# Routing of two token tiles: residual stream and statistics per half, and a gate ahead of the second half of the first tile's routing

## The chip, the cores and the metric

One core of one Trainium2 chip runs the kernel. The metric is device time in microseconds of one execution, median of three runs. Instructions of one engine run in the order in which the program lists them; the engines (TensorE = PE, VectorE = DVE, ScalarE = ACT, GpSimd = POOL, SyncE = SP, which issues the weight loads) wait for one another by semaphores.

## The reference, cut to what matters

256 tokens pass two hybrid layers and then a block with a state-space branch, a pooling branch, and a mixture of experts. The change lies between the block's output projection and its experts:

```python
xl = post_norm(xl, mod_l[2] * out_l, ln1_g, ln1_b)      # layer_norm(ALPHA * x + gate * out)
hl = modulate(xl, mod_l[3], mod_l[4]).reshape(b * l, d)
lg = hf @ w_rg + b_rg                                   # 4 group logits
grp = argmax(lg)
le = (hf @ w_re[grp]) + b_re[grp]                       # 8 expert logits of that group
top_v, top_i = top_k(le, 2)                             # two experts per token
```

Each token then goes through its two experts out of 32 (1024 to 512 to 1024), and the weighted sum is added to the stream.

## The kernel before, in words

The tokens lie in two tiles of 128 partitions, t = 0 and t = 1, and every product of 1024 output columns is cut in two halves of 512, n = 0 and n = 1.

**Output projection (in `mix`, "wout").** Four accumulators `po[t][n]` take the four PSUM buffers of pool `pa`. After the first half of the reduction is done for all four, the rest comes tile by tile: t = 0 with n = 0 and n = 1, then t = 1 with n = 0 and n = 1. Each of the four is 4 calls of `mm3`, and one `mm3` is 3 matmuls of 512 columns.

**Routing (`pre`, one task per tile).** Its steps, with the lines that the trace shows:

1. Stream and statistics: per half a product with the gate row (L1881), the sum into the stream (L1882) and `bn_stats` (L1884; L1838 for the second half), then `bn_aggr` and two small operations on DVE (L1839 to L1843) and two on POOL (L1844, L1847), which give 1/sigma and -mean/sigma.
2. Eight transposes of the stream on PE (L337) into two buffers of PSUM pool `pt` (which has two), four copies to SBUF on ACT (L1892), and a small product on DVE (L1895).
3. The logits: 8 float32 matmuls (the trace shows 16 passes, `pb_wout` for t = 0, `pb_pre` for t = 1); then the normalised stream (L1903 on DVE for t = 0, L1901 on ACT for t = 1), its rounded copy (L1904, ACT) and, for t = 0, the remainder (L1937, DVE).
4. `route`: the first maximum and the group (L1954 to L1972), then the second maximum (L1963 again, to L1976). L1975 writes the assignment `Asg`.
5. Slots and gather: `Asg` matmuls for the positions (`pt_pre`, `pb_pre`), then L1920 and L2029 on DVE make the selection matrix, and 16 matmuls of 256 columns (`pa_pre`) gather the tile's tokens into four accumulators that reuse the buffers of `po`. After those of t = 1 the result is copied out (L2094, L2096), and the experts begin (`pb_moe`, L2124).

**What sets the order.** The instructions are listed by a small planner at build time. A task is a Python generator; `self.clk` counts planned PE time; `yield c` makes the task due `c` units later, and `poll`, at the end of every `mm3`, lets each due task list its next step. `join` goes on with the task that is due first until the named one is done. `YPRE = (2.0, 1.3, 0.6, 0.2)` are the delays behind the steps 1, 2 and 3 and in the middle of `route` (the last two for t = 0 alone). In these units an `mm3` counts 0.64, a transpose 0.21, and a logits matmul 0.107. The dictionary `self.sc` gets a tile's statistics at the end of step 3, and task 0 stands before its step 5 until tile 1's are there (`while 1 not in self.sc: yield 0.5`). A buffer goes to a new tile once the last use of the old one, as listed, is over.

**Behind it.** `pre_end` computes the weights of the experts. Then 16 pairs of experts follow, each with 12 weight blocks of 1 MB that SP streams through a ring of buffers; a load is listed when the matmuls that free its buffer are. SP's queue is in order too.

Of the kernel before, what the change touches and what calls it, by code (L numbers as in the profile page):

```python
# [13 lines left out]
OP = mybir.AluOpType  # L14
# [13 lines left out]
ALPHA = 2.0 ** 0.25  # L28
# [26 lines left out]
YPRE = (2.0, 1.3, 0.6, 0.2)  # L55
# [179 lines left out]
class Emit:  # L235
# [214 lines left out]
    def m(self, n=512, dt=F32):  # L450

        self.n += 1
        return self.mp.tile([P, 512], dt, tag="m", name=f"m_{self.n}")[:, :n]
# [1122 lines left out]
    def mix(self):  # L1576
        nc, A, m = self.nc, self.A, self.m
# [149 lines left out]
        for k, u in MIX_ORDER:  # L1727
# [19 lines left out]
            if u < 8 and u % 2:  # L1747
                g = u // 2
# [8 lines left out]
        po = [[self.pA() for _ in range(2)] for _ in range(2)]  # L1757
        for j in range(8):
# [6 lines left out]
            for i in range(2):  # L1765
                hi, lo = self.half(("vba", j), i)
                for k in range(8):
                    kk = 8 * i + k
                    c = slice(k * P, (k + 1) * P)
# [14 lines left out]
        tp = []  # L1784
        for t in range(2):
            sl = slice(t * P, (t + 1) * P)
            for n in range(2):
                for k in range(4):
                    hi, lo = w[2 * n + k // 2]
                    c = slice((k % 2) * 512, (k % 2 + 1) * 512)  # L1790
                    self.mm3(po[t][n], mx.h(4 + k)[:, sl], mx.l(4 + k)[:, sl], hi[:, c], lo[:, c], False, k == 3)
            tp.append(self.spawn(self.pre(po, t)))
        self.done(4)
        self.prefetch(RING_C + NSPL)
        self.ph = "pre"
# [54 lines left out]
    def pre_start(self):  # L1850

        m, small = self.m, self.small
        self.yT = [m().rearrange("p (k s) -> p k s", k=2) for _ in range(4)]
        self.nh, self.nl = ([self.a4(n, F32R) for _ in range(2)] for n in ("yh", "yl"))
        self.G, self.posm = (self.mw.tile([P, 2, 32], F32, name=n) for n in ("G", "posm"))
        self.asg = self.mw.tile([P, 2, 32], F32R, name="Asg")
        self.mxc = self.mw.tile([P, 1], I32, name="mxc")

        r = self.rt = m(512)

        nc, self.rows = self.nc, r[:, 384:512]
        nc.gpsimd.memset(self.rows, 0.0)
        nc.gpsimd.dma_start(self.rows[0:16], self.A["rows"][4:6, :].rearrange("a (k p) -> (a k) p", p=P))
        nc.gpsimd.dma_start(self.rows[16:24], self.md_dram[1])
        self.gl, self.el, self.v0, self.v1, self.gmx, self.og = (
            r[:, a:b].rearrange("p (t e) -> p t e", t=2) for a, b in ((0, 8), (8, 72), (72, 80), (80, 88), (88, 90), (90, 98)))
        self.o = [r[:, a:a + 64].rearrange("p (t e) -> p t e", t=2) for a in (98, 162)]
        self.rc, self.rb, self.rg = (r[:, a:b].rearrange("p (t e) -> p t e", t=2) for a, b in ((226, 290), (290, 362), (362, 380)))  # L1870
        self.Q0 = m(dt=F32R).rearrange("p (t s) -> p t s", t=2)
        self.sc = {}

    def pre(self, po, t):

        nc, x = self.nc, self.x[t]
        st = self.small(2, 6)
        for n in range(2):
            c = slice(n * 512, (n + 1) * 512)
            g = self.m()  # L1880
            nc.vector.tensor_tensor(g, po[t][n], self.gate_row[:, c], op=OP.mult)  # L1881
            nc.vector.scalar_tensor_tensor(x[:, c], x[:, c], ALPHA, g, op0=OP.mult, op1=OP.add)  # L1882
            if n == 0:
                nc.vector.bn_stats(st[:, 0, :], x[:, c])  # L1884
        nm, r = sc = self.stats_end(st, x[:, 512:])
        yield YPRE[0]
        for q in range(2):
            ps = self.pT()
            for k in range(4):
                self.tr(ps[:, k * P:(k + 1) * P], x[:, (4 * q + k) * P:(4 * q + k + 1) * P])  # L1890
            for k in range(2):
                nc.scalar.activation(self.yT[2 * q + k][:, :, t * P:(t + 1) * P],  # L1892
                                     ps[:, 2 * k * P:2 * (k + 1) * P].rearrange("p (k s) -> p k s", k=2), AF.Copy)

        nc.vector.scalar_tensor_tensor(self.rb[:, t], self.wsum, nm, self.rsm[:, R_BR:R_BR + 36], op0=OP.mult, op1=OP.add)  # L1895
        yield YPRE[1]
        pl = self.pB()
        for k in range(8):
            self.mm(pl[:, :36], self.yT[k // 2][:, k % 2, t * P:(t + 1) * P], self.vr[:, k * 36:(k + 1) * 36], k == 0, k == 7)
        if t:  # L1900
            nc.scalar.activation(x, x, AF.Identity, scale=r, bias=nm)  # L1901
        else:
            nc.vector.tensor_scalar(x, x, r, nm, op0=OP.mult, op1=OP.add)  # L1903
        nc.scalar.activation(self.nh[t], x, AF.Copy)  # L1904
        if t == 0:
            self.low_part(t)
        self.sc[t] = sc
        yield YPRE[2] if t == 0 else 0.0
        yield from self.route(t, pl, r)
        if t == 0:  # L1910
            while 1 not in self.sc:
                yield 0.5
            self.pn, self.pp = self.pB(), self.pT()
            self.mm(self.pp[:, 0:32], self.sbr, self.asg[:, 0])
            self.mm(self.pp[:, 32:64], self.onr, self.asg[:, 0], True, False)
            self.mm(self.pn[:, 0:32], self.onr, self.asg[:, 0], True, False)
        else:
            self.mm(self.pp[:, 32:64], self.sbr, self.asg[:, 1], False, True)
            self.mm(self.pn[:, 0:32], self.onr, self.asg[:, 1], False, True)
        nc.vector.tensor_tensor(self.posm[:, t], self.posm[:, t], self.pp[:, 32 * t:32 * t + 32], op=OP.add)  # L1920
        self.slots(0, (t,), self.Q0)
        if t:
            self.low_part(t)
        if t == 0:
            self.xg0 = self.slots_input()
            self.pg = [self.pA() for _ in range(4)]
        for y in (self.nh, self.nl):
            for k in range(8):
                kb = slice(k * P, (k + 1) * P)
                o = self.pg[k // 2][:, k % 2 * S:(k % 2 + 1) * S]  # L1930
                self.mm(o, y[t][:, kb], self.Q0[:, t], t == 0 and y is self.nh and k % 2 == 0, t == 1 and y is self.nl and k % 2 == 1)
                if t and y is self.nl and k % 2:
                    for i in (k - 1, k):
                        self.channels(self.xg0(i), self.pg[k // 2][:, i % 2 * S:(i % 2 + 1) * S], i)
# [4 lines left out]
    def route(self, t, ps, r):  # L1939

        nc = self.nc
        tt, stt, red = nc.vector.tensor_tensor, nc.vector.scalar_tensor_tensor, nc.vector.tensor_reduce

        def g4(v):
            return v.rearrange("p (g e) -> p g e", e=8)

        def b8(v):
            return v[:, :, None].to_broadcast([P, 4, 8])

        rb, gl, el = self.rb[:, t], self.gl[:, t], g4(self.el[:, t])  # L1950
        c, b, cg, bg = g4(self.rc[:, t]), self.rg[:, t, 0:4], self.rg[:, t, 4:8], self.rg[:, t, 8:9]
        gmx, og = self.gmx[:, t], self.og[:, t]
        o = [g4(x[:, t]) for x in self.o]
        stt(self.el[:, t], ps[:, 4:36], r, rb[:, 4:36], op0=OP.mult, op1=OP.add)  # L1954
        stt(gl, ps[:, 0:4], r, rb[:, 0:4], op0=OP.mult, op1=OP.add)

        group = [lambda: red(gmx, gl, axis=AX.X, op=OP.max),
                 lambda: tt(cg, gl, gmx.to_broadcast([P, 4]), op=OP.is_equal),
                 lambda: stt(cg, cg, -64.0, self.io8[:, 0:4], op0=OP.mult, op1=OP.add),
                 lambda: red(bg, cg, axis=AX.X, op=OP.min),  # L1960
                 lambda: tt(og, cg, bg.to_broadcast([P, 4]), op=OP.is_equal)]
        for i, v in enumerate((self.v0[:, t], self.v1[:, t])):
            for f in (lambda: red(v, el, axis=AX.X, op=OP.max),  # L1963
                      lambda: tt(c, el, b8(v), op=OP.is_equal),
                      lambda: stt(c, c, -64.0, self.io8[:, None, :].to_broadcast([P, 4, 8]), op0=OP.mult, op1=OP.add),
                      lambda: red(b, c, axis=AX.X, op=OP.min),
                      lambda: tt(o[i], c, b8(b), op=OP.is_equal)):
                f()
                if group:
                    group.pop(0)()  # L1970
            if i == 0:
                stt(el, o[0], -3e38, el, op0=OP.mult, op1=OP.add)  # L1972
                yield YPRE[3] if t == 0 else 0.0
        tt(c, o[0], o[1], op=OP.add)
        tt(g4(self.asg[:, t]), c, b8(og), op=OP.mult)  # L1975
        nc.vector.tensor_scalar(self.posm[:, t], self.asg[:, t].bitcast(F32), -1e6, 1e6, op0=OP.mult, op1=OP.add)  # L1976
# [425 lines left out]
```

## Time and profile before

| what | value |
|---|---|
| runs | 1620.33 us median of 3 (1618.15 to 1621.02) |
| profiled execution | 1620.23 us, span 1618.5 us |
| PE busy | 1534.4 us, 95% of the span |
| DVE busy | 938.1 us, 58% |
| ACT busy | 641.3 us, 40% |
| moved from HBM | 406.15 MB, 253 GB/s over the span |
| stretch of the change | from about 1107 to 1135 us of the span |

The span is the part of the execution in which instructions ran; 1.73 us of the profiled execution lie outside it. A row of the timeline gives start, time from the first start to the last end of the merged instructions, engine, line, operation, output and inputs, count, and in brackets the idle time of the engine before it with what ended that. A line such as L330 or L337 is that of a helper; the name of the output tells what it was called for.

### The profile page before, as it was taken

The page shows a single profiled execution, that of the slowest core. Times are in us where ns is not written, and L with a number is a line of the kernel's source. Part 1 is how long each engine was busy: PE and PEld are TensorE (multiplying, and loading weights), DVE is VectorE, ACT ScalarE, POOL GpSimd, SP SyncE. Part 2 cuts the span into 40 slices and gives each one's busy share as a digit, 9 for nine tenths or more (in the row PEclk, how much of TensorE's full clock was granted, in tenths as well). Part 3 has the DMA queues.
Part 4 walks back from the last instruction along what each step waited for, and adds up shares of the span by engine and source line. Part 5 has one row for each costly group of instructions (what it writes and reads, how often), then busy time and mean ns, then how long its engine had stood idle before and what let it go on. Part 6 is the DMA issues. An engine that isn't in the chain of part 4 may idle for free.

```text
span 1618.5 us, 23434 instructions
## 1 busy us (share of the span) xinstructions
PE 1534.4 (95%) x9319; PEld 1172.6 (72%) x9319; DVE 938.1 (58%) x1670; ACT 641.3 (40%) x1103; POOL 37.8 (2%) x55
## 2 busy tenths in 40 slices
PE   7999999999999999998899999998999999989886
PEld 6888999999889999998777779997544444434332
DVE  6768787658777777579899875466321112111103
ACT  5646544446556444456545545442211111111100
POOL 1000000000000000000000000000000000000000
PEclk9999999999999999999999999998999999999998
DMA  8655666644455666644433235588699999999996
GB/s 331 225 197 220 221 231 248 242 172 156 138 176 181 228 227 254 224 150 160 167 124 114 98 117 183 192 315 325 236 365 410 411 410 411 412 412 410 411 412 245
DMA packets 90251, 411.16 MB, mean 254 GB/s; under 512 B 10520, under 2 KB 15568, under 8 KB 62216
## 3 DMA queue, kind: packets, MB, share of 16 engines
q1 hardware_dynamic: 83032, 401.12, 65.6%
q0 software_dynamic: 2464, 6.37, 1.2%
q10 hardware_dynamic: 4640, 2.12, 0.4%
q8 instruction: 75, 1.23, 0.3%
q14 instruction: 40, 0.33, 0.1%
HBM read 406.15 MB, written 3.94 MB: 253 GB/s over the span
## 4 chain that ended last, share of the span: by engine, by line
PE 70%; DVE 13%; DMA 12%; ACT 2%; issue 2%; POOL 1%; SPq 0%; DVEq 0%; ACTq 0%; POOLq 0%
PE pb_ff L330 16%; PE pb_moe L2124 10%; PE pa_ff L330 8%; PE pa_z L330 7%; PE pb_gate L330 4%; DMA w<-in_weu_dram 4%; DMA w<-in_wed_dram 4%; PE pb_moe L2174 3%; DVE lo L376 3%; PE pb_br L330 3%; DMA w<-in_weg_dram 2%; DVE m L1267 2%; PE pa_zz L330 2%; PE pa_uu L330 2%; PE pa_wo L330 2%
## 5 line engine op out<-in xcount | busy, mean ns | idle before, releaser
L376 DVE TENSOR_TENSOR lo<-raw,hi 128x1024 fp32r<-128x1024 f32 (+2 forms) x334 | 383.6, 1165 | 31.3 <-ACT hi L389 31.2
L389 ACT ACTIVATE hi<-raw 128x1024 fp32r<-128x1024 f32 (+2 forms) x334 | 335.4, 1008 | 143.7 <-PE pa_z L330 46.1
L2124 PE MATMUL pb_moe<-w,xg 128*64 128x512 f32 x960 | 240.1, 596 | 10.5 <-DMA w<-in_weg_dram 10.3
L330 PE MATMUL pb_ff<-hh,hi 128*128 128x256 f32 x704 | 200.6, 285 | 0.0
L330 PE MATMUL pb_ff<-hl,hi 128*128 128x256 f32 x704 | 199.1, 283 | 0.0
L330 PE MATMUL pb_ff<-hh,lo 128*128 128x256 f32 x704 | 199.1, 283 | 0.0
L2124 PEld LDWEIGHTS pb_moe<-w,xg 128*64 128x64 f32 x960 | 74.3, 137 | 140.3 <-issue 108.9
L470 ACT ACTIVATE m<-m 128x256 fp32r<-128x256 f32 (+1 forms) x76 | 38.3, 504 | 282.9 <-DVE m L2180 184.7
L330 PEld LDWEIGHTS pb_ff<-hh,hi 128*128 128x128 f32 x704 | 134.7, 191 | 1.1
L330 PEld LDWEIGHTS pb_ff<-hl,hi 128*128 128x128 f32 x704 | 134.7, 191 | 1.0
L330 PEld LDWEIGHTS pb_ff<-hh,lo 128*128 128x128 f32 x704 | 134.7, 191 | 0.0
L2174 PE MATMUL pb_moe<-w,m 128*64 128x512 f32 x472 | 120.8, 596 | 12.4 <-DMA w<-in_wed_dram 12.3
L2094 DVE TENSOR_SCALAR xg<-pt_moe,rsm 128x256 f32<-128x256 f32 x28 | 13.9, 540 | 182.1 <-PE pt_moe L2159 182.1
L330 PE MATMUL pa_ff<-hi,m 128*128 128x512 f32 x352 | 116.0, 397 | 0.0
L2174 PEld LDWEIGHTS pb_moe<-w,m 128*64 128x64 f32 x472 | 38.6, 137 | 83.2 <-issue 54.8
L330 PE MATMUL pa_z<-hi,hh 128*128 128x384 f32 (+1 forms) x256 | 94.5, 369 | 0.2 <-ACT hi L389 0.2
L330 PE MATMUL pa_z<-lo,hh 128*128 128x384 f32 (+1 forms) x256 | 88.9, 347 | 0.3 <-DVE lo L376 0.3
L1267 DVE SCALAR_TENSOR_TENSOR m<-m,fx 128x254 f32<-128x254 f32 (+1 forms) x176 | 85.0, 483 | 7.0 <-ACT m L1255 2.1
L330 PE MATMUL pa_z<-hi,hl 128*128 128x384 f32 (+1 forms) x256 | 88.6, 346 | 0.0
L330 PEld LDWEIGHTS pa_ff<-hi,m 128*128 128x128 f32 x352 | 66.2, 188 | 15.1
L330 PE MATMUL pa_ff<-lo,m 128*128 128x512 f32 x176 | 70.0, 397 | 0.0
L2180 DVE TENSOR_TENSOR m<-pb_moe,gm 128x512 f32<-128x512 f32 x31 | 21.4, 692 | 81.9 <-PE pb_moe L2174 78.8
(539 smaller groups left out, 3001.0 us busy)
## 6 DMA issues: line engine op xcount, KB each, us to landing
raw<-in_wgu_dram SPq DMA_DIRECT2D x44, 1024.0 KB, 5.3
w<-in_wed_dram SPq DMA_DIRECT2D x84, 512.0 KB, 10.2
w<-in_weu_dram SPq DMA_DIRECT2D x82, 512.0 KB, 9.0
w<-in_weg_dram SPq DMA_DIRECT2D x78, 512.0 KB, 10.2
raw<-in_vx_dram SPq DMA_DIRECT2D x22, 1024.0 KB, 5.0
raw<-in_wdn_dram SPq DMA_DIRECT2D x22, 1024.0 KB, 4.9
raw<-in_wza_dram SPq DMA_DIRECT2D x27, 768.0 KB, 4.6
w<-in_weg_dram SPq DMA_DIRECT2D x20, 1024.0 KB, 13.8
```

Source lines behind the costliest of these rows:

```text
L330: self.nc.tensor.matmul(out, l, r, start=start, stop=stop)
L376: self.nc.vector.tensor_tensor(lo, src, hi.bitcast(F32), op=OP.subtract)
L389: self.nc.scalar.activation(hi, s, AF.Copy)
L470: self.nc.scalar.activation(hi, src, AF.Copy)
L1267: nc.vector.scalar_tensor_tensor(acc[:, o0:o1], u[:, o0 + d:o1 + d], w, acc[:, o0:o1], op0=OP.mult, op1=OP.add)
L2094: self.nc.vector.tensor_scalar(dst, src, g, b, op0=OP.mult, op1=OP.add)
L2124: self.nc.tensor.matmul(ps[64 * i:64 * i + 64, :], xg(kk)[:, o + 64 * i:o + 64 * i + 64], w[i][k], start=kk == 0, stop=kk == 7)
L2174: self.nc.tensor.matmul(pd[64 * i:64 * i + 64, :], fT[:, k * P + 64 * i:k * P + 64 * i + 64], w[i][k], start=k == 0, stop=k == 3)
L2180: self.nc.vector.tensor_tensor(yg, pd, self.gm[:, n * 512:(n + 1) * 512], op=OP.mult)
```

## The change

The stream and statistics of step 1 become a function `pre_half`, which is listed behind the matmuls of each half instead of once behind both. The second maximum of tile 0 is listed only when `self.sc` has an entry of tile 1, and that entry is now written when tile 1's statistics are listed (end of step 1), no longer at the end of step 3. The test before step 5 of tile 0 is unchanged in its text.

```diff
                     self.mm3(po[t][n], mx.h(4 + k)[:, sl], mx.l(4 + k)[:, sl], hi[:, c], lo[:, c], False, k == 3)
-            tp.append(self.spawn(self.pre(po, t)))
+                self.pre_half(po, t, n)
+            tp.append(self.spawn(self.pre(t)))
...
+    def pre_half(self, po, t, n):
+        nc, c = self.nc, slice(n * 512, (n + 1) * 512)
+        g, xv = self.m(), self.x[t][:, c]
+        nc.vector.tensor_tensor(g, po[t][n], self.gate_row[:, c], op=OP.mult)
+        nc.vector.scalar_tensor_tensor(xv, xv, ALPHA, g, op0=OP.mult, op1=OP.add)
+        if n == 0:
+            self.st[t] = self.stats_begin(xv)
+
+    def pre(self, t):
         nc, x = self.nc, self.x[t]
-        st = self.small(2, 6)
-        for n in range(2):
-            c = slice(n * 512, (n + 1) * 512)
-            g = self.m()
-            nc.vector.tensor_tensor(g, po[t][n], self.gate_row[:, c], op=OP.mult)
-            nc.vector.scalar_tensor_tensor(x[:, c], x[:, c], ALPHA, g, op0=OP.mult, op1=OP.add)
-            if n == 0:
-                nc.vector.bn_stats(st[:, 0, :], x[:, c])
-        nm, r = sc = self.stats_end(st, x[:, 512:])
+        nm, r = self.sc[t] = self.stats_end(self.st[t], x[:, 512:])
         yield YPRE[0]
...
         if t == 0:
             self.low_part(t)
-        self.sc[t] = sc
         yield YPRE[2] if t == 0 else 0.0
         yield from self.route(t, pl, r)
...
             if i == 0:
                 stt(el, o[0], -3e38, el, op0=OP.mult, op1=OP.add)
-                yield YPRE[3] if t == 0 else 0.0
+                while t == 0 and 1 not in self.sc:
+                    yield 0.2
```

## Rows read from the trace of the kernel before

**Rows 1.** The page's part on the chain that ended last, by engine.
```profile
PE 70%; DVE 13%; DMA 12%; ACT 2%; issue 2%; POOL 1%; SPq 0%; DVEq 0%; ACTq 0%; POOLq 0%
```

**Rows 2.** Stretches of 10 us: busy time by engine, then clock, DMA share, GB/s.
```profile
1130.00:1140.00 10.00, 9.26 (x57) 6.30 (x58) 7.75 (x31) 3.07 (x8) 0.00 (x0) 0.94 0.26 77
...
1150.00:1160.00 10.00, 8.53 (x61) 5.96 (x61) 5.33 (x8) 1.19 (x2) 0.00 (x0) 1.00 0.11 41
...
1180.00:1190.00 10.00, 10.00 (x48) 3.31 (x46) 2.67 (x4) 0.63 (x1) 0.00 (x0) 1.00 0.83 247
...
1370.00:1380.00 10.00, 7.42 (x35) 2.29 (x33) 2.77 (x4) 1.26 (x2) 0.00 (x0) 1.00 1.03 402
```

**Rows 3.** Waits of SP's queue, 1080 to 1618 us: total, times, longest.
```profile
SPq L2081 <- PE pb_moe L2124: 29.6, 21, 10.3
```

**Rows 4.** The chain of waits in order of time: start, length, what.
```profile
1115.73 1.72 PE pb_wout L330 x16
...
1123.68 3.26 PE pb_pre L330 x16
...
1128.08 3.55 PE pa_pre L330 x16
...
1132.49 2.25 PE pa_pre L330 x16
1134.74 3.61 PE pb_moe L2124 x16
```

**Rows 5.** Timeline of DVE, 1107 to 1131 us.
```profile
1107.38 0.69 DVE L1881 TENSOR_TENSOR m<-pa_br,gm 128x512 f32<-128x512 f32 x1 [0.40 <-PE pa_br L330]
...
1113.82 0.81 DVE L1903 TENSOR_SCALAR x<-x,sm,sm 128x1024 f32<-128x1024 f32 x1
1115.75 1.23 DVE L1937 TENSOR_TENSOR yl<-x,yh 128x1024 fp32r<-128x1024 f32 x1 [1.13 <-ACT yh L1904]
1117.47 0.25 DVE L1954 SCALAR_TENSOR_TENSOR m<-pb_wout,sm,m 128x32 f32<-128x32 f32 x1 [0.50 <-PE pb_wout L330]
...
1118.99 0.68 DVE L1881 TENSOR_TENSOR m<-pa_br,gm 128x512 f32<-128x512 f32 x1
...
1121.05 0.67 DVE L1881 TENSOR_TENSOR m<-pa_br,gm 128x512 f32<-128x512 f32 x1
...
1123.58 0.18 DVE L1963 TENSOR_REDUCE m<-m 128x4 f32<-128x32 f32 x1
...
1124.93 0.19 DVE L1975 TENSOR_TENSOR Asg<-m 128x32 fp32r<-128x32 f32 x1
...
1127.38 0.19 DVE L1920 TENSOR_TENSOR posm<-posm,pt_pre 128x32 f32<-128x32 f32 x1 [1.88 <-PE pt_pre L330]
...
1127.94 0.25 DVE L1954 SCALAR_TENSOR_TENSOR m<-pb_pre,sm,m 128x32 f32<-128x32 f32 x1
...
1130.92 0.19 DVE L1975 TENSOR_TENSOR Asg<-m 128x32 fp32r<-128x32 f32 x1
```

**Rows 6.** Timeline of PE, 1112 to 1127 us.
```profile
1112.63 1.04 PE L337 MATMUL pt_wout<-cp,x 128*128 128x128 f32 x8
...
1120.55 0.71 PE L337 MATMUL pt_pre<-cp,x 128*128 128x128 f32 x4 [2.34 <-DVE x L1882]
1122.59 1.09 PE L337 MATMUL pt_pre<-cp,x 128*128 128x128 f32 x4 [1.34 <-DVE x L1882]
...
1126.75 0.59 PE L330 MATMUL pt_pre<-Asg,m 128*128 128x32 f32 x2
```

**Rows 7.** Timeline of ACT: the copies behind the first four transposes of tile 1.
```profile
1121.29 0.66 ACT L1892 ACTIVATE m<-pt_pre 128x256 f32<-128x256 f32 x2 [5.57 <-PE pt_pre L337]
```

**Rows 8.** Stretches of 2 us, the columns of rows 2 (clock third from the end).
```profile
1120.00:1122.00 2.00, 0.71 (x4) 0.42 (x4) 1.93 (x4) 0.66 (x2) 0.00 (x0) 0.74 1.02 418
...
1126.00:1128.00 2.00, 1.55 (x8) 1.44 (x7) 0.59 (x3) 0.87 (x1) 0.00 (x0) 0.50 1.03 412
...
1130.00:1132.00 2.00, 1.75 (x11) 1.65 (x10) 1.41 (x8) 0.00 (x0) 0.00 (x0) 0.70 0.00 0
```

More of the change, by code (lines that the diff above doesn't have):

```diff
@@ L1871, in pre_start @@
         self.Q0 = m(dt=F32R).rearrange("p (t s) -> p t s", t=2)
-        self.sc = {}
-    def pre(self, po, t):
-        nc, x = self.nc, self.x[t]
-        st = self.small(2, 6)
-        for n in range(2):
-            c = slice(n * 512, (n + 1) * 512)
-            g = self.m()
-            nc.vector.tensor_tensor(g, po[t][n], self.gate_row[:, c], op=OP.mult)
-            nc.vector.scalar_tensor_tensor(x[:, c], x[:, c], ALPHA, g, op0=OP.mult, op1=OP.add)
-            if n == 0:
-                nc.vector.bn_stats(st[:, 0, :], x[:, c])
-        nm, r = sc = self.stats_end(st, x[:, 512:])
+        self.sc, self.st = {}, {}
+    def pre_half(self, po, t, n):
[6 more added lines that the diff above has]
+    def pre(self, t):
+        nc, x = self.nc, self.x[t]
+        nm, r = self.sc[t] = self.stats_end(self.st[t], x[:, 512:])
         yield YPRE[0]
```

## The prediction, made before the changed kernel was built or timed

> **What bounds the kernel now.** I read the page first. The chain that ended last runs through PE for 70%, DVE 13%, DMA 12% [rows 1], so a stage counts only where it holds PE up or the weight loads. Then the stretches of 10 us [rows 2]: from 1130 to 1140 the loads move 77 GB/s and from 1150 to 1160 only 41, although 32 experts are still to be fetched, and 247 between 1180 and 1190; by 1370 they run at 402 GB/s, 1.03 of the engines' time, while PE falls to 7.42 of 10 us. So the last part is bound by the loads, but the loads themselves stand still when the experts begin. Why, SP's waits tell [rows 3]: 29.6 us in 21 waits for expert matmuls (L2124), up to 10.3 at once. All buffers are full, and none comes free before the experts' matmuls run. The chain by time gives that start: behind the gather of tile 1 (1132.49, 2.25 us) the experts begin at 1134.74 [rows 4]. Whatever moves 1134.74 moves every later release of a buffer, hence the end, one for one.
>
> The stretch before it is a chain over PE, DVE and ACT. PE waits 2.34 us and 1.34 us for tile 1's stream halves (L1882) [rows 6], does its transposes and its logits, and gathers tile 0 (1128.08, 3.55 us [rows 4]) while DVE routes tile 1: L1954 at 1127.94, `Asg` at 1130.92 + 0.19 = 1131.11 [rows 5]. That gather costs nothing before: it lies beside the route.
>
> **Part 1: tile 0's halves listed earlier.** Nothing. L1881 of tile 0 already starts at 1107.38 on the signal of PE alone [rows 5]; no other work of DVE was listed between the two places.
>
> **Part 2: tile 1's first half listed earlier.** Planned time puts it behind tile 0's transposes, before tile 0's normalised stream. Its three DVE operations take 1121.05 - 1118.99 = 2.06 us [rows 5]. Its matmuls are over when PE begins tile 0's transposes at 1112.63 [rows 6], so DVE runs them at 1113.82, where L1903 stood. L1903, and through ACT's rounded copy L1937, go from 1115.75 to 1117.81; with 1.23 us of L1937, tile 0's route (L1954) starts at 1119.0, not 1117.47: 1.5 later. From there the first half of the route takes 1118.99 - 1117.47 = 1.52, so tile 1's second half starts at 1120.5 and takes 1123.58 - 1121.05 = 2.53 with its statistics; tile 0's second maximum starts at 1123.05 instead of 1123.58, and its `Asg` (1124.93 + 0.19 before) is ready at 1124.6 [rows 5]. By itself a gain of 0.5 us, since the DVE work is the same and only a wait of DVE's (0.50 in the row at 1117.47, and part of that at 1115.75) is used.
>
> **Part 3: the gate.** Before, the test reads: go on when tile 1's logits have been listed. Step through it after the change. Tile 0's route is listed at the last `mm3` and yields, as `self.sc` has no entry 1. Then tile 1's second half and statistics are listed, and the entry is written there. The joins begin with task 0: due 0.2 after, against 2.0 for task 1. It lists its second maximum, as before. But the next test, before step 5, now passes too: the entry is there. So the `Asg` matmuls, L1920, L2029 and all 16 gather matmuls of tile 0 are listed *before* tile 1's transposes and logits. No DMA is moved past anything. On PE tile 1's eight transposes stand behind matmuls that wait for `Asg` of tile 0, and DVE's route of tile 1 waits for PE. In times:
>
> - `Asg` at 1124.6. The `Asg` matmuls start at 1126.75 and L1920 at 1127.38 in the rows, 0.63 [rows 6, 5]; so L1920 at 1125.25. From L1920 to the gather 1128.08 - 1127.38 = 0.70: gather at 1125.95, 3.55 long at the low clock: PE free at 1129.5. Until then PE has been idle since 1120.55 - 2.34 = 1118.2, over 6 us.
> - Tile 1's transposes. The position buffer `pp` now holds one of the two `pt` buffers until tile 1's slots, so the second four wait for ACT's copies of the first four. Low clock: 0.71 + 0.66 [rows 6, 7] and, as an estimate from the gaps 1120.55 + 0.71 to 1121.29, 0.1 of signals, then 1.09: 1132.05. High clock: 1.04 for eight [rows 6], so 0.52 + 0.76 + 0.52: 1131.3.
> - Logits: 3.26 low, 1.72 high [rows 4]: 1135.3 or 1133.0. PE does this while nothing else is left to do on DVE.
> - Route of tile 1: 1131.11 - 1127.94 = 3.17 to `Asg` [rows 5], 0.63 to L1920, 0.70 to the gather: 4.5 us with PE idle. Gather at 1139.8 or 1137.5.
> - Gather of tile 1: 3.55 low, 2.25 high [rows 4]. Experts at 1143.4 or 1139.75, against 1134.74: +8.7 or +5.0.
>
> The unknown is the clock. [...] Transposes and logits, though PE was busy with them, did not bring it back; it came back 3.1 us into the gather. If the new gather of tile 0 does so too, at 1129.05, the transposes and logits are high, but PE then stands idle from 1133.0 on for 4.5 us; before, 2.8 us after PE fell idle it was low. So the last gather is low: 5.0 + 1.3 = +6.3. If the 3.5 us of gather are not enough, it is +8.7. As a further bound, the experts' first matmuls may start low: before, the low level lasted 8.6 us from the work at 1122.59; less the gather's 3.55, 5 us at half rate cost 2.5: +11.2. The lower bound is +5.0, all high. I take +7.5, the middle of 6.3 and 8.7, the two that the rows of this same stretch support.
>
> [...]
>
> **Sum.** 1620.23 (profiled execution: 1618.5 of span and 1.73 around it) + 7.5 = 1627.7. It lies 0.1 us under the runs' median of 1620.33, which changes nothing. Behind 1134.74 the order of the experts and their loads is the same, and the loads' standstill grows by the same 7.5 us.
>
> **Rivals.**
>
> *The order stays* (the change does only what its words say: tile 0's gather is still listed behind tile 1's logits). For it: the test's text is unchanged, and a gather ahead of the transposes is not named. Against it: the entry in `self.sc` is written before both tests. Then tile 1's first transposes run at 1118.2 instead of 1120.55, the second ones start when the second L1882 ends, 0.55 earlier than 1122.59 because L1881 moves from 1121.05 to 1120.5, and the logits, `Asg` and gathers follow: -0.6; if the earlier transposes also kept the clock high, 1.5 on the logits (3.26 against 1.72) and 1.3 on the gather, of which the route of tile 1 hides the latter: -2.1. 1619.6, down to 1618.1. This is the case on the other side: no loss, decided by whether the second test passes. The same would come if PE took ready matmuls past waiting ones: the transposes would slip ahead whatever the list says. [...]
>
> *The loads absorb the delay.* For it: from 1370 the loads run without a pause and PE waits for them [rows 2]. If they had something to fetch while PE is late, the end would not move: 1620.3. Against it: 77 and 41 GB/s at 1130 to 1160, and SP waiting for expert matmuls [rows 2, 3]; they have no free buffer. To absorb half, 3.7 us: 1624.
>
> *The clock decides otherwise.* All high 1625.2, low far into the experts 1631.4: my own range.
>
> **How the numbers follow.** Forecast with its clock bounds 0.88, order stays 0.08, loads absorb 0.04. The likeliest is 1627.7, its range 1624.5 to 1630.5: it leaves out the far end of the clock and the two rivals with no loss, together under 0.2. A difference below 0.2%, 3.2 us, cannot be told from none here. Slower by more: 0.88 and half of the absorbed case, less a little for a forecast at its very lowest, 0.88. Within: 0.09. Faster by more: 0.03, if the order stays and the clock gives back more than I count.
>
> **What would show it.** Right: on PE the first `pa_pre` matmuls stand before `pt_pre` transposes of tile 1; PE idle some 6 us behind `pa_br`, and again about 4 us before the second `pa_pre`; L1954 of tile 1 between 1133 and 1135.5; the experts begin at 1139.8 to 1143.4; the loads idle that much longer, and the later stages are shifted alike. Part 2 is right if L1954 of tile 0 stands near 1119.0 and `Asg` of tile 0 near 1124.6. Wrong: transposes of tile 1 at 1118; experts at 1134; or a late start with the end unmoved.

## The result and the profile after

The changed kernel takes 1628.77 us (median of 7 runs, 1626.03 to 1631.52) against 1620.33 for the kernel before (7 runs): the ratio is 1.0052, interval 1.0039 to 1.0066, some 8.4 us slower. The forecast was 1627.7, slower, with a chance of 0.88. The profiled execution took 1631.4 us with a span of 1629.6; it is one of the longest of the seven.

The chain of waits of the changed kernel, in order of time (start, length, what):

```profile
1125.85 3.75 PE pa_pre L330 x16
1129.60 0.87 PE pt_pre L337 x4
1130.49 0.67 ACT m L1894 x2
1131.21 1.12 PE pt_pre L337 x4
1132.32 3.27 PE pb_pre L330 x16
...
1140.07 3.75 PE pa_pre L330 x16
1143.82 4.42 PE pb_moe L2126 x16
```

Tile 0's gather now stands ahead of tile 1's transposes and logits, each on the path by itself; in [rows 4] the logits came first and the gather lay beside DVE's route. The experts begin at 1143.82 instead of 1134.74. PE and DVE by the timeline of the changed kernel:

```profile
1112.40 1.04 PE L337 MATMUL pt_wout<-cp,x 128*128 128x128 f32 x8
...
1124.45 0.58 PE L330 MATMUL pt_pre<-Asg,m 128*128 128x32 f32 x2 [6.46 <-DVE Asg L1977]
...
1131.21 1.12 PE L337 MATMUL pt_pre<-cp,x 128*128 128x128 f32 x4 [0.75 <-ACT m L1894]
...
1138.85 0.39 PE L330 MATMUL pt_pre<-Asg,m 128*128 128x32 f32 x1 [3.27 <-DVE Asg L1977]
```

```profile
1113.60 0.68 DVE L1879 TENSOR_TENSOR m<-pa_br,gm 128x512 f32<-128x512 f32 x1
...
1118.72 0.24 DVE L1955 SCALAR_TENSOR_TENSOR m<-pb_wout,sm,m 128x32 f32<-128x32 f32 x1
...
1124.11 0.19 DVE L1977 TENSOR_TENSOR Asg<-m 128x32 fp32r<-128x32 f32 x1
...
1135.62 0.25 DVE L1955 SCALAR_TENSOR_TENSOR m<-pb_pre,sm,m 128x32 f32<-128x32 f32 x1 [9.75 <-PE pb_pre L330]
```

The waits have changed sides. PE is idle 6.46 us for tile 0's assignment and 3.27 us for tile 1's; DVE is idle 9.75 us for tile 1's logits, where in [rows 5] its longest wait was 1.88 us and tile 1's L1954 came close behind tile 0's L1920. The first four transposes of tile 1 were ready in those 6.46 us: in e1 below they run at 1117.30. PE did not take them past the matmuls that waited, so the prediction's aside that it might is out. Now the stretches, of 2 us and of 10 us (columns of rows 2, clock third from the end):

```profile
1120.00:1122.00 2.00, 0.00 (x0) 0.00 (x0) 1.93 (x6) 0.00 (x0) 0.00 (x0) 0.90 1.03 416
...
1130.00:1132.00 2.00, 1.25 (x7) 0.85 (x6) 0.00 (x0) 0.66 (x2) 0.00 (x0) 0.50 0.00 0
...
1144.00:1146.00 2.00, 2.00 (x8) 0.50 (x8) 1.70 (x10) 0.93 (x4) 0.00 (x0) 0.63 0.04 8
```

```profile
1130.00:1140.00 10.00, 5.45 (x25) 4.80 (x23) 3.80 (x24) 3.50 (x6) 0.00 (x0) 0.50 0.00 0
1140.00:1150.00 10.00, 9.93 (x46) 6.28 (x48) 5.91 (x23) 3.27 (x9) 0.00 (x0) 0.73 0.28 80
...
1160.00:1170.00 10.00, 8.53 (x59) 5.84 (x60) 5.33 (x8) 1.20 (x2) 0.00 (x0) 1.00 0.11 34
```

The granted clock is 0.50 from about 1121.6 (0.90 in the first row) to 1145.5 (0.63 in the third). The loads do nothing at all from 1130 to 1140 (0 GB/s), and the pattern of [rows 2], 77, then 41 GB/s at 1150, stands ten later: 80, then 34 at 1160.

### The profile page after: what moved, and what is told of

Its sections match the earlier page's. It is cut to its first block, busy times and chain, and to the rows that moved or that the text cites. A ratio compares the mean times of both kernels' runs of the same rounds, so it can differ in the third digit from the quotient of the medians.

```text
span 1629.6 us, 23435 instructions
## 1 busy us (share of the span) xinstructions
PE 1539.0 (94%) x9319; PEld 1176.5 (72%) x9319; DVE 937.7 (58%) x1670; ACT 641.6 (39%) x1103; POOL 38.0 (2%) x55
## 4 chain that ended last, share of the span: by engine, by line
PE 64%; DMA 19%; DVE 13%; ACT 2%; issue 1%; POOL 0%; SPq 0%; DVEq 0%; ACTq 0%; POOLq 0%
PE pb_ff L330 16%; DMA w<-in_weu_dram 8%; PE pa_z L330 8%; PE pa_ff L330 7%; PE pb_moe L2126 6%; DMA w<-in_wed_dram 6%; PE pb_gate L330 4%; DMA w<-in_weg_dram 4%; PE pb_br L330 3%; DVE lo L376 3%; DVE m L1267 2%; PE pa_wo L330 2%; PE pa_zz L330 2%; PE pa_uu L330 2%; PE pb_xs L330 1%
```

## The experiments

Each was timed beside the kernel before, the first four on one chip, the last two on another. The stage is measured within each profile, from the first transposes of tile 0 to the experts' piece of the chain, since the stages ahead of it differ by a microsecond or two between executions.

| kernel | ratio to before | interval | stage, us |
|---|---|---|---|
| before | | | 1134.74 - 1112.63 = 22.1 |
| changed | 1.0052 | 1.0039 to 1.0066 | 1143.82 - 1112.40 = 31.4 |
| e1, test put back | 0.9997 | 0.9989 to 1.0006 | 1133.66 - 1111.88 = 21.8 |
| e2, gate alone | 1.0059 | 1.0044 to 1.0073 | 1141.80 - 1112.10 = 29.7 |
| e3, changed, PE filled | 1.0026 | 1.0017 to 1.0035 | 1139.77 - 1114.24 = 25.5 |
| e4, e1 with 11 matmuls | 1.0003 | 0.9994 to 1.0011 | 1133.74 - 1111.98 = 21.8 |
| e5, e1 with 20 matmuls | 0.9982 | 0.9973 to 0.9991 | 1132.12 - 1112.52 = 19.6 |
| e6, before, 40 matmuls ahead of the experts | 1.0065 | 1.0049 to 1.0081 | 1145.03 - 1113.66 = 31.4 |

**e1: the halves as changed, the second test as before** (`lgt` is a new set, empty at first).

```diff
+        self.lgt.add(t)                     # behind the logits of tile t, where sc was written before
         yield YPRE[2] if t == 0 else 0.0
...
-            while 1 not in self.sc:
+            while 1 not in self.lgt:
                 yield 0.5
             self.pn, self.pp = self.pB(), self.pT()
```

Expected:

> The halves listed early as in the change, but tile 0's gather waits again until tile 1's logits are listed. Theory (the order of the gather on PE is the whole loss): experts start near 1134.0 us of the span, 0.7 before the kernel before, time 1619.6 us, ratio to before 0.9996, not to be told from before. Rival (delaying tile 0's normalised stream and route by 1.2 to 1.5 us is what costs): the time stays above before by that 1.5 us or more, up to the changed kernel's 1628.8.

Measured 1619.65 us, ratio 0.9997: the whole loss is gone. PE of e1:

```profile
1111.88 1.04 PE L337 MATMUL pt_wout<-cp,x 128*128 128x128 f32 x8
...
1117.30 0.60 PE L337 MATMUL pt_pre<-cp,x 128*128 128x128 f32 x4
1121.27 1.09 PE L337 MATMUL pt_pre<-cp,x 128*128 128x128 f32 x4 [3.37 <-DVE x L1880]
1122.15 3.47 PE L330 MATMUL pb_pre<-vr,m 128*128 128x36 f32 x16
...
1126.75 2.07 PE L330 MATMUL pa_pre<-m,yh 128*128 128x256 f32 x8 [0.53 <-DVE m L2032]
```

Transposes, logits, gather, as in [rows 6, 4]. The rival, that tile 0's later normalised stream costs, falls: the displaced operations are here and cost nothing that the time shows. What the early halves gain, 0.3 us in the stage, is below what the time can show.

**e2: the kernel before with the entry written early, nothing else.**

```diff
-        nm, r = sc = self.stats_end(st, x[:, 512:])
+        nm, r = self.sc[t] = self.stats_end(st, x[:, 512:])
...
-        self.sc[t] = sc
```

Expected:

> The kernel before with one thing changed: the statistics entry is written when tile 1's statistics are listed, so tile 0's gather is listed ahead of tile 1's transposes; the halves stay where they were. Theory: nearly the whole loss, and 0.5 more since tile 0's assignment comes 0.5 later: experts near 1144.3, time 1629.3 us, ratio 1.0055. Rival (the moved halves cost): about 1620.3, ratio 1.000.

Measured 1629.07 us, ratio 1.0059: this line is enough for the loss. The profiled execution of e2 is one of the faster ones (span 1625.3); its experts begin at 1141.80, not at the 1144.3 expected. Its chain, and one stretch with the clock, show why:

```profile
1126.15 3.75 PE pa_pre L330 x16
...
1132.16 1.72 PE pb_pre L330 x16
...
1138.37 3.43 PE pa_pre L330 x16
1141.80 3.58 PE pb_moe L2123 x16
```

```profile
1131.00:1132.00 1.00, 0.50 (x4) 0.50 (x5) 0.00 (x0) 0.45 (x2) 0.00 (x0) 0.98 0.00 0
```

The order is that of the changed kernel, but here the clock came back at about 1131.0 (0.98 in the row), in time for the logits (1.72, not 3.27), and was low again in tile 1's gather (3.43). So e2's profile met the 6.3 us case of the forecast and the changed kernel's profile the 8.7 one. That the spread between their runs comes from this is likely, but each has one profile only.

**e3: the changed kernel with PE kept at work.**

```diff
+    def pe_fill(self, n):
+        d = self.pT()
+        for _ in range(n):
+            self.nc.tensor.matmul(d, self.idr, self.nh[0][:, :512], start=True, stop=True)
...
         nm, r = self.sc[t] = self.stats_end(self.st[t], x[:, 512:])
+        if t:
+            self.pe_fill(24)
...                                          # behind the logits
+            self.pe_fill(12)
```

Expected:

> The changed kernel with 24 matmuls of 512 columns put on PE behind the last output projection, and 12 behind tile 1's logits; nobody reads them. [...] Theory with a clock share: logits 3.27 to 1.72, the two gathers 3.75 to 2.25 each, transposes about 0.7 less, experts' first matmuls 0.9 less: 5.5 to 6 less, experts near 1138.5, time 1623 us, ratio 1.0017; what is left of the loss, about 3 to 5 us, is the order alone. Rival (the order alone is the loss and the clock has no share): 1628.8, ratio 1.005.

Measured 1623.65 us, ratio 1.0026, where 1.0017 was expected. The granted clock was 1.00 throughout, and the chain has these lengths:

```profile
1118.00:1128.00 10.00, 8.50 (x45) 6.87 (x45) 7.64 (x32) 1.06 (x1) 0.75 (x2) 1.00 0.99 390
1128.00:1138.00 10.00, 8.14 (x56) 6.95 (x55) 4.37 (x24) 3.50 (x6) 0.00 (x0) 1.00 0.30 120
```

```profile
1127.40 2.17 PE pa_pre L330 x16
1129.58 0.45 PE pt_pre L337 x4
1130.05 0.67 ACT m L1896 x2
1130.76 0.66 PE pt_pre L337 x4
1131.42 1.72 PE pb_pre L330 x16
...
1137.51 2.26 PE pa_pre L330 x16
1139.77 3.60 PE pb_moe L2135 x16
```

The added matmuls do no useful work, yet they give back 0.0026 of the 0.0052: at the high clock the changed kernel is 4.2 us behind the kernel before (2.8 to 5.7). That is not yet the price of the order, since the kernel before pays for the low clock too. The like-for-like pair is e3 and e5 below, both at a granted clock of 1.00 throughout: 1.0026 against 0.9982, some 7 us (5 to 9 by their intervals), and 25.5 against 19.6 us in the stage. Without added matmuls the pair is the changed kernel and e1, both with a stretch at 0.50: 1.0052 against 0.9997, some 9 us (6 to 11), and 31.4 against 21.8 in the stage. So most of the loss is the order by itself; the clock adds 3.7 us by the stages of these profiles and about 2 by the times, which is within their noise.

**e4: e1 with 11 such matmuls between the two fours of tile 1's transposes.**

```diff
         for q in range(2):
+            if t and q:
+                self.pe_fill(11)
             ps = self.pT()
```

Expected (the first kernel is e1, and the theory takes the granted clock to stay at 1.00 with these matmuls):

> [...] Theory: logits 1.72 instead of 3.26 and gather of tile 0 2.25 instead of 3.55, after which DVE sets the pace: experts near 1132.4, 2.3 before the kernel before, time 1618 us, ratio 0.9986. Rival (DVE alone sets the chain here, the clock changes nothing): as the first kernel, 1619.6.

Measured 1620.04 us, ratio 1.0003: a miss. The clock of e4 by stretches, its logits, and the chain:

```profile
1118.00:1122.00 4.00, 3.21 (x18) 2.39 (x17) 3.90 (x18) 0.66 (x2) 0.00 (x0) 1.00 1.03 420
1122.00:1124.00 2.00, 1.69 (x16) 1.59 (x16) 1.73 (x11) 1.35 (x3) 0.75 (x2) 0.93 1.03 416
1124.00:1128.00 4.00, 3.45 (x15) 3.36 (x16) 3.38 (x23) 1.61 (x2) 0.00 (x0) 0.50 1.03 410
```

```profile
1121.82 1.87 PE L330 MATMUL pb_pre<-vr,m 128*128 128x36 f32 x16
```

```profile
1125.34 3.78 PE pa_pre L330 x16
...
1129.98 3.75 PE pa_pre L330 x16
1133.74 3.71 PE pb_moe L2135 x16
```

The logits ran at a granted clock of 1.00 (1.87 us in this view, 3.47 in e1), but it fell to 0.50 at about 1123.7 (0.93 in the second row), behind them, and both gathers ran low: what the logits gained the second gather lost (3.75 against 2.26 in e1). The low stretch was moved, not removed, so this run did not yet tell my theory from the rival.

**e5: 14 matmuls there, 2 behind tile 1's logits, 2 ahead of each gather** (the edit of e4 with 14, and two more lines `pe_fill(2)`, one of which serves both gathers).

Expected:

> As the kernel with the gather back behind the logits and 11 idle matmuls, with 14 of them there, 2 more behind tile 1's logits, and 2 ahead of each gather. In the run with 11 the clock fell to half at 1123.9, behind the logits, and both gathers ran at 3.75 us. Theory (the clock was still the pace there): if it now stays up, the gathers take 2.25, DVE's route of tile 1 sets the pace, and the experts begin 1.8 us earlier than in that run: ratio 0.9988, 1617.7 us. If logits lower the clock whatever stands around them, it falls again and nothing is gained: ratio 1.000. Rival (PE's order and clock have nothing left to give here): no gain although the clock stays up.

Measured 1617.44 us, ratio 0.9982, interval 0.9973 to 0.9991: faster than both kernels. The clock of e5 and the end of its chain:

```profile
1118.00:1128.00 10.00, 9.66 (x62) 7.87 (x60) 9.28 (x48) 3.62 (x6) 0.75 (x2) 1.00 1.02 414
1128.00:1138.00 10.00, 9.09 (x52) 5.33 (x54) 7.38 (x30) 3.59 (x11) 0.00 (x0) 1.00 0.45 141
```

```profile
1128.51 0.20 DVE Asg L1988
1128.71 0.04 issue
1128.76 0.30 PE pt_pre L330
...
1129.87 2.25 PE pa_pre L330 x16
1132.12 3.61 PE pb_moe L2137 x16
```

At a granted clock of 1.00 throughout, tile 1's assignment sets the pace (DVE), and the stage takes 19.6 us, 2.2 less than e1's. So the low clock was what held e1, by some 2.4 us of its time (0.9997 against 0.9982).

**e6: the kernel before with PE late at the experts.** 40 such matmuls at the head of `pre_end`, behind tile 1's gather.

Expected:

> The kernel before with 40 matmuls of 512 columns that nobody reads, between tile 1's gather and the experts: PE reaches the experts 9.1 us later (40 at 0.227), at full clock, and nothing else changes. Theory (whatever the experts' start loses, the end loses): 1628.7 us, ratio 1.0056. Rival (the loads, which PE waits for at the end, take a part of a late start in): less than 1.004.

Measured 1630.02 us, ratio 1.0065. The matmuls took 9.35 us of the chain:

```profile
1133.42 2.26 PE pa_pre L330 x16
1135.68 9.35 PE pt_pre L1940 x40
1145.03 3.58 PE pb_moe L2131 x16
```

0.0065 of 1620 us is 10.5, interval 7.9 to 13.1: the 9.35 us come out at the end, in full as far as the times can tell. The loads take in 1.4 us of a late start at most, although PE waits for them at the end (7.42 us of 10 busy from 1370 [rows 2]).

## Why the prediction was right

**What bounds the stage.** A late start of the experts moves the end one for one: shown by e6 (9.35 us of late start, 7.9 to 13.1 us of time), and by the profiles, where the pattern of the loads is the same and ten microseconds later. That rival had 0.04 and is out.

**Part 1** was counted at nothing, and tile 0's first L1879 starts on PE's signal as L1881 did. **Part 2**: the three DVE operations start at 1113.60, tile 0's route at 1118.72 (forecast 1119.0), its `Asg` is written at 1124.11 + 0.19 = 1124.3 (forecast 1124.6); the stage's first row is 0.23 earlier in this execution, so both agree. That it costs nothing by itself is e1's result; the 0.5 us that it should gain is 0.3 in e1's stage and not seen in its time.

**Part 3, the gate.** The step that carried the forecast: the entry is there before the second test, so the gather is listed ahead. The orders on PE show it, e1 undoes it and with it all the loss, and e2 makes the loss with it alone. The terms at the low clock against the profile: tile 0's gather 3.55, measured 3.75 (the row of before held a little of the high clock at its end); the transposes with ACT's copies between them 1129.5 to 1132.05, measured 1129.60 to 1132.32; logits 3.26, measured 3.27; L1955 of tile 1 at 1135.3, measured 1135.62; experts at 1143.4, measured 1143.82. With the stage's start 0.23 earlier the terms fell short by 0.65: 0.2 for each gather, nearly 0.2 for the transposes (the 0.71 of [rows 6] was in part at the high clock; four take 0.87 at the low one). The wait for one of two PSUM buffers is the 0.75 us that PE waits for ACT.

One reading was off without harm to the sum. The gather of before is said to cost nothing beside DVE's route. At the low clock the gather outlasted the route: 1128.08 + 3.55 = 1131.63 [rows 4], `Asg` at 1131.11. In e5, at a granted clock of 1.00, the gather ended first, at 1127.81, and PE waited 0.94 us for `Asg`, written at 1128.71; that is a part of what e5 gains.

**The clock**, the term with ends far apart, was taken at 7.5, between 6.3 and 8.7. The forecast's 3.1, 2.8 and 8.6 us count from a granted clock that before fell from 1.00 to 0.50 at about 1121.0 and came back at about 1131.2, as stretches of a quarter of a microsecond show (columns of rows 2):

```profile
1120.75:1121.00 0.25, 0.25 (x4) 0.19 (x2) 0.25 (x1) 0.00 (x0) 0.00 (x0) 0.93 1.08 442
...
1131.00:1131.25 0.25, 0.25 (x4) 0.25 (x3) 0.22 (x2) 0.00 (x0) 0.00 (x0) 0.59 0.00 0
```

The changed kernel's profile had 0.50 up to the experts and paid 0.8 us more in the first experts' matmuls (4.42 against 3.61 in [rows 4]), which stood only in the outer bound; e2's profile had the other case. The median of 8.4 lies between them, but its interval, 6.3 to 10.7 us, holds both. So that the forecast came within 1.1 us is in part luck: 7.5 was the middle of two cases, and no row chose it. The lower bound, +5.0, was called all high, but has tile 0's gather at 3.55; e3, at 1.00 throughout, measured 4.2. In the changed kernel PE worked from 1125.85 to 1130.47 without a pause and the granted clock stayed at 0.50; the case of +6.3 is that of e2's profile alone.

**What stays open.** The profiled execution is 11.1 us longer in span than that of before, 9.1 by the start of the experts and 0.8 by their first matmuls. The remaining 1.2 us appear behind 1336, where PE comes to wait for the loads: the expert pair at 1335.90 before is 9.78 late, as those ahead of it are, and the one at 1393.22 is 10.79 late. In e6's profile the same stretch takes 1.3 us off (10.15 late, then 8.88), so this looks like spread between executions; one profile of each does not settle it. It also stays open why the clock came back in e2's profile and not in that of the changed kernel.

## What to carry to other kernels

When a flag is written earlier so that one test passes, look for every other test of the same flag: here the second one put 16 matmuls that wait for DVE ahead of work that was ready, and PE stood idle for 6.46 us rather than take that work first. Gather or output work that hides beside another engine's chain must be listed behind the work that feeds that chain: the stage took 21.8 us so (e1) and 31.4 the other way. Where two engines took turns here, the clock granted to PE also fell, to 0.50 from 1121.6 to 1145.5. Matmuls that nobody reads gave 2.4 us back on the good order and 4.2 on the bad one, less than the 7 us of the order itself, and only where the level stayed up to the end of the stretch (e5, not e4). And whoever splits a loss into causes must free both kernels of the other cause: e3 against the kernel before shows 4.2 us for the order, e3 against e5 some 7.

## What the runs showed of the hardware

The granted clock fell in e4 from 1.00 to 0.50 at about 1123.7, although PE had worked on four transposes and the logits without a pause since 1121.36; in e5, with three more matmuls of 512 columns ahead of these and two behind, it did not fall. In the changed kernel it did not rise from 0.50 in 4.6 us of gather and transposes (1125.85 to 1130.47), nor in the transposes and logits that followed 0.75 us later. In e2 the same order met a rise to 1.00 at about 1131.0. The same stretch of work thus ran at either level in the profiles of two kernels, with 1.5 us on the logits alone (3.27 against 1.72).
